# The opening of a hybrid decoder step: step sizes in two passes with high and low weights side by side, products four k tiles behind, warm-up products on a constant, banks and turns regrouped

## The chip, the cores and the metric

One Trainium2 chip, one of its cores. The time is device microseconds of one execution of the whole kernel: 2484.97 before the change, the median of three runs between 2484.46 and 2486.34.

## What is computed

One layer of a decoder that has three token mixers (a gated convolution, a Mamba-2 scan, a cross-attention into 256 memory tokens) behind one input projection, and a SwiGLU block behind them. A prompt of 1024 tokens and eight sample tokens go through the same weights. The part that this case touches is the beginning: the norm of x, its product with the columns of w_in for the step sizes dt (32 heads), for B and C and the gates z, and the norm of the memory.

```python
mem_n = rmsnorm(mem_prompt, norm_mem_w[l])
mk = (mem_n @ w_mem_k[l]).reshape(bp, MEM_LEN, ATTN_HEADS, ATTN_HEAD_DIM)
...
sc_b, sc_c, sc_x, z, xbc, dt_raw, q, gates = jnp.split(xn @ w_in, splits, axis=-1)
xbc_c, ssm_conv_new = causal_depthwise_conv(xbc, ssm_hist, ssm_conv_w)
xbc_c = jax.nn.silu(xbc_c + ssm_conv_b)
xs, bm, cm = jnp.split(xbc_c, [SSM_D_INNER, SSM_D_INNER + SSM_GROUPS * SSM_STATE], axis=-1)
dt = jax.nn.softplus(dt_raw.astype(jnp.float32) + ssm_dt_bias.astype(jnp.float32))
a = -jnp.exp(ssm_a_log.astype(jnp.float32))
acum = jnp.cumsum((dt * a).reshape(bsz, nc, q, ng, hpg), axis=2)
```

## The kernel before

All products are f32 in value: every operand is split into a high part in the format fp32r and a low part (the rest, fp32r as well), and a product is three passes over PE, high x high, high x low and low x high. A weight block is 128 columns of w_in by 1024 rows, loaded as one tile of 128 x 1024 (tag raw), cast to high by ACT (whi) and subtracted to low by DVE (wlo). The names end in r, h and l: wdtr, wdth, wdtl. The activations xn are eight k tiles (128 rows of the model dimension) of 1032 tokens, xnh and xnl, and every product over all tokens comes as three column groups of 256, 512 and 264 (FULL).

**The order** on each engine is fixed when the program is built: a scheduler walks the program in the order in which it is written, each engine then works through its own queue in order, and semaphores tie the queues together. The loads and stores of SP have eight semaphores in turn, so each waits for the one eight places earlier. Where the program calls `in_turn`, the casts, the subtractions and the loads of weights stay in the order in which they are written.

**The opening**, to which the change belongs:

1. Constants: ident, ones (128 x 128 in f32, L94), tri.
2. Three of the eight x tiles are loaded, then the small parameter rows, then the weights of dt (wdtr, L493; 128 columns are loaded although dt has 32 heads) and of B0 (wB0r), then the other x tiles.
3. `square` and `root_of`: sums of squares by ACT, the inverse root by DVE and ACT, spread over partitions by PE (ps_rb) and copied to rbc.
4. A loop over three token groups (384, 384, 264 tokens) and eight k tiles. `blocks` transposes x into ps_xt (PE, L529), and `to_xn` copies it to xt (ACT, L510; three buffers), sends xt to xT_d in DRAM (SP, L511), scales it to xw (DVE, L513), casts xnh (ACT, L514) and subtracts xnl (DVE, L515). `first_products` adds the products of dt and B0 into ps_dt and ps_B, for token group g - 1 while group g is transposed; each k tile has six products, three for dt and three for B0.
5. Behind the loop: the histories of the convolutions are transposed (ps_h) and copied (h_xc, h_sc); the first linear combination for the later Strassen products is cast (T10ah, T10al, L406); ps_dt gets its bias and becomes dtr (DVE, L606); ps_B is copied to uB (ACT, L794); then `gemm` writes ps_C (C0), and `z_step(0)` and `z_step(1)` write ps_z, each followed by a silu on ACT (z, L815).
6. `gemm` calls `tick` several times in a product of 24 x 3 matmuls; `pace[0]` (3) says how many times. Each tick takes the next piece of a list, `pend`: the softplus of dt (`dt_softplus`, transposes ps_dtT), cumulative sums ps_ac (L647), their transposes ps_acT with the exponentials eaT (L669), the rows of the sample (ps_ex, L690), the norm of the memory (`mem_rms`), its transposes (`mem_t`, ps_mt, L1241: two pieces of two halves each, each half with four transposes and then four casts and four subtractions), the keys and values (`kv_block`).
7. From Z2 on, pairs of column blocks are computed by `strassen` (L302) in seven products of half the size, with `st_prod` (L261), in three PSUM tiles with the tags m0, m1 and m2. Z2 and Z4 are the first two.

PSUM has eight banks. ps_dt, ps_B and each ps of a gemm take three banks; m0, m1 and m2 two banks each. A tile waits for whoever last used its banks.

```python
tags = ("m0", "m1", "m2") if count[0] % 2 == 0 else ("m2", "m1", "m0")
...
pa, pb = (st_ps(t, f"{nm}{t}") for t in tags[:2])
...
n = int(pace[0] + pace[1])
pace[1] += pace[0] - n
marks = [nk * i // n for i in range(n)]
```

## Time and profile before

| | |
|---|---|
| median of three runs | 2484.97 us |
| the profiled execution | 2481.99 us, its span 2480.1 us |
| busy share of PE, PEld, DVE, ACT, POOL | 98%, 93%, 64%, 43%, 5% |
| granted clock of PE, mean over the span | 0.996 |
| PE busy in 0 to 60 us | 0.81, 6.80, 8.08, 8.87, 10.00 and 9.26 of each 10 |
| PE busy in 160 to 280 us | 120.00 of 120 |

PE is matmul, PEld weight load, DVE the vector engine, ACT the scalar engine, POOL gpsimd, SP the queue of loads and stores. The profile is read stage by stage: the busy share of PE says little about the first 160 us, which are the only ones in which PE waits for other engines. In a row of the timeline stand the start and the length of a run of like instructions, the engine, the line, the operation, the output, the inputs, the shape and their number; in brackets stands the idle time ahead of it and what ended it. The table of windows gives busy time by engine, and the chain of waits names what was last at each step.

### The profile page before, as it was taken

How to read it: one execution, taken by the hardware profiler on the slowest of the kernel's cores; microseconds unless marked ns; L12 is line 12 of the kernel's file. 1: busy time of each engine (PE TensorE's matmuls, PEld its weight loads, DVE VectorE, ACT ScalarE, POOL GpSimd, SP SyncE). 2: the span in 40 equal slices, each digit the busy share in tenths (PEclk: the TensorE clock that was granted, in tenths of full speed). 3: DMA queues.
4: the chain of work that ended last, by engine and by line, in shares of the span. 5: the costliest groups of instructions: out<-in, count | busy, mean ns of one | idle time of the engine just before them, and what ended most of it. 6: DMA issues, size and time to landing. Idle time of an engine off the chain costs nothing.

```text
span 2480.1 us, 45608 instructions
## 1 busy us (share of the span) xinstructions
PE 2426.3 (98%) x18906; PEld 2308.0 (93%) x18906; DVE 1587.2 (64%) x2598; ACT 1072.3 (43%) x1716; POOL 118.3 (5%) x163
## 2 busy tenths in 40 slices
PE   7999999999999999999999989999999999999998
PEld 5899999999999999888888877899999999999998
DVE  5754587777678774656767562454787555476755
ACT  6553455454555535556545441213453333342322
...
GB/s 199 107 128 171 121 104 154 126 114 120 136 129 140 128 160 205 182 207 262 264 225 286 205 257 236 256 249 154 133 176 145 99 95 112 69 224 144 154 86 69
DMA packets 359661, 404.80 MB, mean 163 GB/s; under 512 B 16422, under 2 KB 286870, under 8 KB 359447
## 3 DMA queue, kind: packets, MB, share of 16 engines
...
## 4 chain that ended last, share of the span: by engine, by line
PE 86%; DMA 6%; DVE 4%; ACT 2%; issue 1%; SPq 0%; ACTq 0%; POOL 0%; DVEq 0%
PE po L215 12%; PE pm L1755 4%; PE ps_q L215 3%; PE pd L215 1%; PE py L998 1%; PE ps_g L215 1%; PE pss L1011 1%; PE po L990 1%; PE Z2m L261 1%; PE C3m L261 1%; PE G18m L261 1%; PE Z14m L261 1%; PE C6m L261 1%; PE G12m L261 1%; PE C4m L261 1%
## 5 line engine op out<-in xcount | busy, mean ns | idle before, releaser
L943 ACT ACTIVATE r<-r,acum 128x128 f32<-128x128 f32 x256 | 79.2, 392 | 4.1 <-DMA r<-ac_d 3.6
L714 DVE SCALAR_TENSOR_TENSOR ax<-u,prm,ax 128x1024 f32<-128x1024 f32 x44 | 56.3, 1280 | 0.1
L975 POOL TENSOR_TENSOR xdd<-xdt,decst 128x512 f32<-128x512 f32 x32 | 38.9, 1215 | 288.8 <-DVE xdt L971 288.8
L884 ACT ACTIVATE st<-st,es 128x128 f32<-128x128 f32 x128 | 41.6, 393 | 22.6 <-DMA st<-in_state_ssm_dram 18.5
L1402 DVE TENSOR_TENSOR yr<-po,yr 128x1032 f32<-128x1032 f32 x8 | 9.8, 1230 | 55.8 <-PE po L215 45.8
L994 DVE TENSOR_TENSOR y<-po,ea 128x512 f32<-128x512 f32 x28 | 19.3, 689 | 37.2 <-PE po L990 37.2
L969 DVE TENSOR_TENSOR r<-r,cbm 128x1024 f32<-128x1024 f32 x32 | 39.2, 1224 | 2.7 <-ACT bT L968 0.5
L886 DVE SCALAR_TENSOR_TENSOR st<-sr,dts,st 128x128 f32<-128x128 f32 x128 | 40.1, 344 | 0.4
L968 ACT COPY bT<-bp 128x128 f32<-128x128 f32 x32 | 8.5, 265 | 69.9 <-DVE cbm L966 69.7
L1989 ACT ACTIVATE fj<-psy 128x512 f32<-128x512 f32 (+1 forms) x18 | 10.7, 595 | 58.9 <-PE psy L1987 58.8
L890 DVE SCALAR_TENSOR_TENSOR sr<-st,sr 128x128 f32<-128x128 f32 x128 | 35.1, 284 | 1.1
L998 PE MATMUL py<-r,xdt 128*64 128x128 f32 x512 | 35.0, 279 | 0.0
L944 ACT ACTIVATE r<-r 128x1024 f32<-128x1024 f32 x32 | 33.8, 1058 | 0.6
L971 DVE TENSOR_TENSOR xdt<-xp,dtT 128x512 f32<-128x512 f32 x32 | 21.9, 685 | 18.6 <-PE xp L964 18.4
L1011 PE MATMUL pss<-xdd,bT 128*128 128x512 f32 x64 | 33.4, 603 | 0.3 <-ACT bT L968 0.3
L1762 DVE TENSOR_TENSOR x<-pm,xT 128x516 f32<-128x516 f32 x16 | 11.1, 695 | 35.1 <-PE pm L1755 35.1
L998 PEld LDWEIGHTS py<-r,xdt 128*64 128x64 f32 x512 | 27.3, 137 | 4.1 <-issue 0.5
L990 PE MATMUL po<-bc,s 128*128 128x128 f32 x224 | 29.8, 276 | 1.0 <-DVE s L1017 1.0
L1024 POOL TENSOR_TENSOR s<-s,cdec 128x512 f32<-128x512 f32 x28 | 30.2, 1078 | 7.4 <-DVE s L1017 7.0
L990 PEld LDWEIGHTS po<-bc,s 128*128 128x128 f32 x224 | 27.6, 191 | 2.8 <-issue 1.6
L1684 DVE TENSOR_TENSOR gt<-po,gt 128x1032 f32<-128x1032 f32 x8 | 9.9, 1232 | 30.0 <-PE po L215 28.2
L717 DVE SCALAR_TENSOR_TENSOR ax<-u,prm,ax 128x1032 f32<-128x1032 f32 x22 | 28.3, 1287 | 0.0
...
## 6 DMA issues: line engine op xcount, KB each, us to landing
...
```

Of the source, the lines that this page charges most:

```text
L215: PE.matmul(out[:, c : c + n], wt[:, ks], x[:, c : c + n], start=(k == 0 and i == 0), stop=(k == nk - 1 and i == 2),)
L261: PE.matmul(hv(ps)[:, c : c + n], wt[:, ks], x[:, c : c + n], start=(start and kt == 0 and i == 0), stop=(kt == 3 and i == 2), skip_group_ ...
L714: V.scalar_tensor_tensor(acc[:, :T], u[:, j : j + T], w[j], acc[:, :T], op0=ALU.mult, op1=ALU.add)
L884: S.activation(st[:, i], st[:, i], AF.Copy, scale=es[:, g * 4 + i, b : b + 1])
L886: V.scalar_tensor_tensor(st[:, i], rb, dts[:, g * 4 + i, b : b + 1], st[:, i], op0=ALU.mult, op1=ALU.add)
L943: S.activation(r[:, j, :], r[:, j, :], AF.Relu, scale=-1.0, bias=acum[:, c, h : h + 1])
L969: V.tensor_tensor(r, r, bc(cbm.unsqueeze(1), [P, HPG, P]), op=ALU.mult)
L975: G.tensor_tensor(b3(xdd, HPG), b3(xdt, HPG), bc(decst[:, c, hs].unsqueeze(2), [P, HPG, 64]), op=ALU.mult)
L990: PE.matmul(po[:, t * P : (t + 1) * P], state["s"][:, t * P : (t + 1) * P], bcg[1][:, cs], start=True, stop=True,)
L998: PE.matmul(py[hp : hp + 64, (h // 2) * P : (h // 2 + 1) * P], xdt[:, h * 64 : (h + 1) * 64], r[:, (h % 2) * 4 + h // 2, :], start=True, s ...
L1011: PE.matmul(pss, bT, xdd, start=True, stop=True)
L1755: PE.matmul(hv(ps)[:, c : c + n], wt[:, ks], x[:, half * HT + c : half * HT + c + n], start=(k == 0 and i == 0), stop=(k == KD - 1 and i = ...
```

## The change

- On PE, 32 products of `ones` with itself (128 x 128, f32) stand ahead of everything else; their result, in a PSUM tile called warm, is not used.
- The weights of dt are loaded with their 32 columns only. High and low stand side by side in one tile, 64 columns per k tile. dt is two passes then, (high and low) x xnh and (high and low) x xnl, and the 64 rows of the result are high and low parts: dtr has 64 rows, the transposes of it are 64 wide (ps_dtT and, for the sample, ps_dtS), and DVE adds the two halves. The result contains the low x low term too, which was left out before. The raw load of B0's weights is issued where it was, their casts follow in `first_weights`, called in the loop at group 0 and k tile 2.
- `first_products` becomes `dt_product` (two matmuls) and `b_product` (three). They are put into a queue, which is taken from with each k tile, from the fifth on: they follow the transposes by four k tiles instead of eight. The B products of the last group stand behind the loop.
- xt has five buffers instead of three.
- The tags of Strassen's tiles: m2, m1, m0 for Z2 (m0, m1, m2 before), m1, m2, m0 for Z4 (m2, m1, m0 before).
- The four halves of `mem_t` are four pieces of `pend` instead of two, and `pace[0]` is 5 during `z_step(1)`, 3 elsewhere.

```diff
--- before.py
+++ after.py
@@ -98,6 +98,10 @@
         base=0, channel_multiplier=-1,
     )
 
+    warm = sm_ps("warm")
+    for _ in range(32):
+        PE.matmul(warm[:, :P], ones, ones, start=True, stop=True)
+
     root = cp.tile([P, 1], F32, tag="root", name="root")
     S.activation(root, ones[:, 0:1], AF.Sqrt)
 
@@ -328,7 +332,12 @@
             raw1, raw2 = lead[0], st_raw(src2, f"{nm}r2")
         elif ready is None and early is None:
             raw1, raw2 = st_raw(src1, f"{nm}r1"), st_raw(src2, f"{nm}r2")
-        tags = ("m0", "m1", "m2") if count[0] % 2 == 0 else ("m2", "m1", "m0")
+        if count[0] == 0:
+            tags = ("m2", "m1", "m0")
+        elif count[0] == 1:
+            tags = ("m1", "m2", "m0")
+        else:
+            tags = ("m0", "m1", "m2") if count[0] % 2 == 0 else ("m2", "m1", "m0")
         count[0] += 1
         pa, pb = (st_ps(t, f"{nm}{t}") for t in tags[:2])
 
@@ -493,8 +502,18 @@
         def par(key, i):
             return prm[:, PC[key] + i : PC[key] + i + 1]
 
-        w_dt = weights(wblock(w_in, C_DT), "wdt")
-        w_b0 = weights(wblock(w_in, C_XBC + 16 * P), "wB0")
+        raw_dt = wp.tile([P, 1024], F32, tag="raw", name="wdtr")[:, : KD * HEADS].rearrange("p (k c) -> p k c", k=KD)
+        in_turn("raw", SY.dma_start(raw_dt, w_in[:, C_DT : C_DT + HEADS].rearrange("(k p) c -> p k c", p=P)))
+        w_b0 = []
+        loaded["wB0"] = load_raw(wblock(w_in, C_XBC + 16 * P), "wB0")
+        w_dt = wp.tile([P, 1024], F32R, tag="whi", name="wdt")[:, : 2 * KD * HEADS]
+        w_dt = w_dt.rearrange("p (k c) -> p k c", k=KD)
+
+        def first_weights():
+            in_turn("hi", S.copy(w_dt[:, :, :HEADS], raw_dt))
+            in_turn("lo", V.tensor_sub(w_dt[:, :, HEADS:], raw_dt, f32(w_dt)[:, :, :HEADS]))
+            w_b0.extend(weights(None, "wB0"))
+
         st = p0.tile([P, 9], F32, tag="st", name="st")
         rst = p0.tile([P, 9], F32, tag="rst", name="rst")
         V.memset(st, 1.0)
@@ -506,7 +525,7 @@
 
         def to_xn(k, c, ps, n, name):
             hi, lo = xn[k]
-            xt = p0.tile([P, 384], F32, tag="xt", bufs=3, name="xt" + name)
+            xt = p0.tile([P, 384], F32, tag="xt", bufs=5, name="xt" + name)
             S.copy(xt[:, :n], ps[:, :n])
             SY.dma_start(xT_d[k, :, c], xt[:, :n])
             xc = xw[k][:, c]
@@ -540,15 +559,27 @@
             c, n_all = span(g3)
             V.tensor_copy(rbc[:, c], ps[:, :n_all])
 
-        def first_products(g3, k):
+        def dt_product(g3, k):
+            cw = slice(FULL[g3][0], sum(FULL[g3]))
+            for i, x in enumerate(xn[k]):
+                PE.matmul(
+                    flat(ps_dt)[: 2 * HEADS, cw], w_dt[:, k, :], x[:, cw],
+                    start=(k == 0 and i == 0), stop=(k == KD - 1 and i == 1),
+                )
+
+        def b_product(g3, k):
             cw = slice(FULL[g3][0], sum(FULL[g3]))
             ah, al = xn[k]
             ks = slice(k * P, (k + 1) * P)
-            for ps, (wh, wl) in ((ps_dt, w_dt), (ps_b0, w_b0)):
-                PE.matmul(flat(ps)[:, cw], wh[:, ks], ah[:, cw], start=(k == 0), stop=False)
-                PE.matmul(flat(ps)[:, cw], wh[:, ks], al[:, cw], start=False, stop=False)
-                PE.matmul(flat(ps)[:, cw], wl[:, ks], ah[:, cw], start=False, stop=(k == KD - 1))
-
+            for i, (w, x) in enumerate(((w_b0[0], ah), (w_b0[0], al), (w_b0[1], ah))):
+                PE.matmul(
+                    flat(ps_b0)[:, cw], w[:, ks], x[:, cw], start=(k == 0 and i == 0), stop=(k == KD - 1 and i == 2)
+                )
+
+        products = deque()
+        for g3 in range(2):
+            products.extend(lambda g3=g3, k=k: [f(g3, k) for f in (dt_product, b_product)] for k in range(KD))
+        products.extend(lambda k=k: dt_product(2, k) for k in range(KD))
 
         for i in range(3):
             square(0, i)
@@ -562,12 +593,16 @@
                 if g3 < 2 and 1 <= k < 1 + len(srcs[g3 + 1]):
                     with tc.issue_after(ins):
                         square(g3 + 1, k - 1)
-                if g3:
-                    first_products(g3 - 1, k)
+                if g3 == 0 and k == 2:
+                    first_weights()
+                if g3 > 0 or k > 3:
+                    products.popleft()()
                 if g3 < 2 and k == 5:
                     root_of(g3 + 1)
+        while products:
+            products.popleft()()
         for k in range(KD):
-            first_products(2, k)
+            b_product(2, k)
 
         SY.dma_start(r_d, rbc[0:1, :])
 
@@ -600,10 +635,11 @@
 
     dt_stack = ExitStack()
     pd_ = dt_stack.enter_context(tc.tile_pool(name="pdt", bufs=1))
-    bias = pd_.tile([HEADS, 1], F32, tag="bias", name="bias")
-    SY.dma_start(bias, a["ssm_dt_bias"].rearrange("l h -> h l"))
-    dtr = ev_tile("dtr", (HEADS, TT))
-    V.tensor_scalar(dtr[:, :TT], flat(ps_dt)[:HEADS], bias, None, op0=ALU.add)
+    bias = pd_.tile([2 * HEADS, 1], F32, tag="bias", name="bias")
+    V.memset(bias, 0.0)
+    SY.dma_start(bias[:HEADS], a["ssm_dt_bias"].rearrange("l h -> h l"))
+    dtr = ev_tile("dtr", (2 * HEADS, TT))
+    V.tensor_scalar(dtr[:, :TT], flat(ps_dt)[: 2 * HEADS], bias, None, op0=ALU.add)
     W = 9 * HEADS
 
     def small(name):
@@ -617,11 +653,17 @@
     def dt_softplus():
         ps = sm_ps("ps_dtT")
         for c in range(NCK):
-            PE.transpose(ps[:, c * HEADS : (c + 1) * HEADS], dtr[:, c * P : (c + 1) * P], ident[:HEADS, :HEADS])
-        PE.transpose(ps[:NS, 256:288], dtr[:, T:TT], ident[:HEADS, :HEADS])
+            PE.transpose(
+                ps[:, c * 2 * HEADS : (c + 1) * 2 * HEADS], dtr[:, c * P : (c + 1) * P], ident[: 2 * HEADS, : 2 * HEADS]
+            )
+        pss = sm_ps("ps_dtS")
+        PE.transpose(pss[:NS, : 2 * HEADS], dtr[:, T:TT], ident[: 2 * HEADS, : 2 * HEADS])
         V.memset(x0[:, 256:], 0.0)
-        V.tensor_copy(x0[:, :256], ps[:, :256])
-        V.tensor_copy(x0[:NS, 256:], ps[:NS, 256:288])
+        for dst, src in ((x0[:, :256], ps), (x0[:NS, 256:], pss[:NS, : 2 * HEADS])):
+            dst = dst.rearrange("p (c h) -> p c h", h=HEADS)
+            src = src.rearrange("p (c t h) -> p c t h", t=2, h=HEADS)
+            V.tensor_copy(dst, src[:, :, 0])
+            V.tensor_tensor(dst, src[:, :, 1], dst, op=ALU.add)
         V.tensor_scalar(mx, x0, 0.0, None, op0=ALU.max)
         V.scalar_tensor_tensor(u, x0, -1.0, x0, op0=ALU.mult, op1=ALU.min)
         S.activation(u, u, AF.Exp)
@@ -1275,9 +1317,11 @@
 
     mem_load()
     pend.extend([None, mem_rms, None])
-    pend.extend(lambda m=m: [mem_t(m, half) for half in range(2)] for m in range(2))
+    pend.extend(lambda m=m, half=half: mem_t(m, half) for m in range(2) for half in range(2))
     pend.extend(lambda j=j, q=q: kv_block(j, q) for j in range(8) for q in range(2))
+    pace[0] = 5
     z_step(1)
+    pace[0] = 3
 
     def plain3():
         for kt in range(4):
```

Where instructions move, and where: first the PE at the beginning of the loop, with the third transposed k tile (three x tiles each into ps_xt) and the first products. Before:

```order
L529 MATMUL ps_xt_238<-ident,x_150 128x128
L529 MATMUL ps_xt_238<-ident,x_152 128x128
L529 MATMUL ps_xt_238<-ident,x_154 128x128
L548 MATMUL ps_dt<-xnh_121,wdth 128x256
L548 MATMUL ps_B_146<-xnh_121,wB0h 128x256
L549 MATMUL ps_dt<-xnl_122,wdth 128x256
L550 MATMUL ps_dt<-xnh_121,wdtl 128x256
L549 MATMUL ps_B_146<-xnl_122,wB0h 128x256
L550 MATMUL ps_B_146<-xnh_121,wB0l 128x256
```

and after (the number in a name tells tiles of one name apart; wdt holds high and low):

```order
L548 MATMUL ps_xt_264<-ident,x_183 128x128
L548 MATMUL ps_xt_264<-ident,x_185 128x128
L548 MATMUL ps_xt_264<-ident,x_187 128x128
L565 MATMUL ps_dt<-xnh_154,wdt 64x256
L565 MATMUL ps_dt<-xnl_155,wdt 64x256
L575 MATMUL ps_B_179<-xnh_154,wB0h 128x256
L575 MATMUL ps_B_179<-xnl_155,wB0h 128x256
L548 MATMUL ps_xt_281<-ident,x_183 128x128
L548 MATMUL ps_xt_281<-ident,x_185 128x128
```

The products of the first k tile stand behind the third transposed tile in both; in the changed program it has two products for dt instead of three, both ahead of B0, and its B0 products are split: low x high comes behind the next tile's transposes.

Second, ACT right behind the loop, where the last xnh are cast and the products of C0 need their weights. Before:

```order
L514 CAST xnh_135<-xw_144 128x264
L163 CAST wz0h<-wz0r 128x1024
L406 CAST T10ah<-xw_137 128x516
L406 CAST T10ah<-xw_138 128x516
L163 CAST wz1h<-wz1r 128x1024
L794 COPY uB_717<-ps_B_146 128x1032
L639 ACT_TABLE_LOAD
L639 ACTIVATE abc<-abc 128x32
```

and after:

```order
L533 CAST xnh_168<-xw_177 128x264
L415 CAST T10ah<-xw_170 128x516
L415 CAST T10ah<-xw_171 128x516
L167 CAST wC0h<-wC0r 128x1024
L167 CAST wz0h<-wz0r 128x1024
L836 COPY uB_726<-ps_B_179 128x1032
L681 ACT_TABLE_LOAD
L681 ACTIVATE abc<-abc 128x32
L753 ACTIVATE aB_730<-uB_726,prm 128x1024
L167 CAST wz1h<-wz1r 128x1024
```

wC0h, cast inside the loop before (at 39.80 us in the profile), now stands behind both casts of T10ah; wz1h has moved behind uB and aB. On SP, the loads wC0r and wz0r stand behind the last xT_d now, and stood among the xT_d of the second and third group before. On DVE, in the same place, before:

```order
L622 MEMSET x_701 128x32
L586 COPY h_xc<-ps_h_0_637 128x192
L586 COPY h_xc<-ps_h_8_649 128x192
L164 TENSOR_TENSOR wz0l<-wz0r,wz0h 128x1024
L586 COPY h_xc<-ps_h_16_661 128x192
L586 COPY h_sc<-ps_h_0_673 128x128
L606 TENSOR_SCALAR dtr<-ps_dt,bias 32x1032
L712 TENSOR_SCALAR aB_721<-h_xc,prm 128x8
L407 TENSOR_TENSOR T10al<-xw_137,T10ah 128x516
```

and after:

```order
L621 COPY h_xc<-ps_h_0_645 128x192
L621 COPY h_xc<-ps_h_8_657 128x192
L621 COPY h_xc<-ps_h_16_669 128x192
L621 COPY h_sc<-ps_h_0_681 128x128
L639 MEMSET bias 64x1
L661 MEMSET x_710 128x32
L416 TENSOR_TENSOR T10al<-xw_170,T10ah 128x516
L416 TENSOR_TENSOR T10al<-xw_171,T10ah 128x516
L168 TENSOR_TENSOR wC0l<-wC0r,wC0h 128x1024
L642 TENSOR_SCALAR dtr<-ps_dt,bias 64x1032
```

dtr now has wC0l and both T10al ahead of it, and in the changed program the first product of C0 on PE waits for dtr and for wC0h; in the program before it waits for uB.

Third, ACT around the silu of z(1), for which the first product of Z2 waits in both programs. Before:

```order
L406 CAST xnh_127<-raw_888 128x516
L669 ACTIVATE eaT<-ps_acT_925 32x512
L815 ACT_TABLE_LOAD
L815 ACTIVATE z_1178<-ps_z_1093 128x1032
L669 ACT_TABLE_LOAD
L669 ACTIVATE eaT<-ps_acT_932 32x512
L816 DMA zs_d<-z_1178 128x1032
L248 CAST Z2Sh<-Z2sa 128x1024
```

and after:

```order
L415 CAST xnh_160<-raw_900 128x516
L711 ACTIVATE eaT<-ps_acT_937 32x512
L711 ACTIVATE eaT<-ps_acT_944 32x512
L857 ACT_TABLE_LOAD
L857 ACTIVATE z_1216<-ps_z_1105 128x1032
L252 CAST Z2Sh<-Z2sa 128x1024
L858 DMA zs_d<-z_1216 128x1032
```

Both eaT stand ahead of z now; one table load is gone between them, and Z2Sh follows z directly. From the third product of Z4 on the order of PE is the same in both programs, as are ACT's and DVE's queues from there.

## The prediction

> **What bounds the kernel now.** I read the table of windows first, because the page's 98% for PE is an average. Its columns are the busy time of PE, PEld, DVE, ACT and POOL in each stretch, then the granted PE clock, the DMA share and GB/s.
>
> ```profile
> 20.00:30.00 10.00, 8.08 (x48) 6.14 (x47) 6.27 (x15) 5.65 (x15) 0.00 (x0) 1.00 0.43 154
> 40.00:50.00 10.00, 10.00 (x52) 7.31 (x51) 8.57 (x19) 5.83 (x14) 0.00 (x0) 1.00 0.70 199
> 100.00:110.00 10.00, 7.37 (x48) 6.90 (x46) 7.05 (x11) 7.24 (x11) 0.00 (x0) 0.83 0.46 133
> 130.00:140.00 10.00, 6.34 (x53) 5.90 (x52) 7.60 (x17) 9.62 (x25) 0.00 (x0) 1.00 0.27 108
> ...
> 160.00:220.00 60.00, 60.00 (x514) 60.00 (x513) 25.90 (x30) 24.14 (x34) 0.00 (x0) 1.00 0.51 161
> ```
>
> PE has holes up to 140 us, and from 160 on it is full: 60.00 of 60. The order of PE differs between the two programs only up to the beginning of Z4 (from the row Z4m<-xnh,Z4Th on it is the same). So the sum is one number, **how much earlier Z4 is reached**, which a PE that waits for nobody carries to the end. The next question is what the holes before Z4 wait for. The chain of waits (start, length, what) names it:
>
> ```profile
> 12.23 1.04 ACT wdth L163
> ...
> 54.94 4.32 DMA xT_d<-xt
> 59.35 1.14 ACT T10ah L406 x2
> 60.50 0.95 ACT wz1h L163
> 61.45 0.92 ACT uB L794
> 62.41 5.53 PE ps_C L215 x18
> 68.85 8.69 PE ps_C L215 x54
> ```
>
> Four points divide the opening: X, the end of the last xt copy on ACT (54.91 before: 54.53 + 0.38 in a row below); the first ps_C product, 62.41, which is X + 7.5; the start of Z2; the start of Z4. The last two rows also show a ps_C product at 0.31 us (5.53 / 18) and then at 0.16 (8.69 / 54): a stretch of PE at half rate, with PE at work all the time.
>
> **Warm products.**
>
> ```profile
> 1.07 0.27 DVE L465 MEMSET rows<- 128x256 f32 x1
> 8.78 0.44 PE L490 MATMUL ps_prm<-ident,rows 128*128 128x128 f32 x1 [8.78 <-DVE rs_v L110]
> 10.79 1.54 PE L529 MATMUL ps_xt<-ident,x 128*128 128x128 f32 x6
> 13.19 0.85 ACT L510 COPY xt<-ps_xt 128x384 f32<-128x384 f32 x2
> 1007.10 1.05 PE L990 MATMUL po<-bc,s 128*128 128x128 f32 x8
> 1008.08 1.09 PE L998 MATMUL py<-r,xdt 128*64 128x128 f32 x16
> ```
>
> The constant is written when the next memset starts, at 1.07, and PE is empty until 8.78. A 128x128 matmul in f32 shows as two rows: eight rows took 1008.08 - 1007.10 = 0.98, so 0.245 us a matmul at full clock. At half clock I take 0.43, since a pair of 256-wide rows goes from 0.24 to 0.43 below. All 32 at full clock end at 1.1 + 7.8 = 8.9, all at half clock at 1.1 + 13.8 = 14.9. The half-rate stretches in this trace last 3.3 to 5.5 us (rows above and below); with 5 us (12 matmuls) and 20 at 0.245 the block ends at **W = 11.0**, the value I take. From ps_prm's start to the xt transposes it is 2.0, half of 1.54 for the first three of them is 0.8, and some 0.2 of waiting for rst falls away: first xt at W + 2.6 = 13.6, **0.4 us later** than 13.19.
>
> **The loop to X.** Each k tile loses one product of ps_dt (five products instead of six).
>
> ```profile
> L510 ACT COPY xt<-ps_xt 128x384 f32<-128x384 f32 (+1 forms) x24 | 10.2, 442 | 8.7 <-PE ps_xt L529 5.6 <-DMA xT_d<-xt 1.5 <-issue 1.3
> 14.45 0.61 DVE L513 SCALAR_TENSOR_TENSOR xw<-ps_xt,prm,rbc 128x384 f32<-128x384 f32 x1
> 15.10 0.51 ACT L514 CAST xnh<-xw 128x384 fp32r<-128x384 f32 x1
> 54.53 0.38 ACT L510 COPY xt<-ps_xt 128x264 f32<-128x264 f32 x1 [0.85 <-PE ps_xt L529]
> ```
>
> At full clock 256 columns cost 0.12 us (the pairs of 0.24 below), 512 twice that, 264 about the same as 256. The 512- and 264-wide products lie where PE is full (10.00 of 10 in 40 to 50): 8 x 0.24 + 8 x 0.12 = **2.9 us**. The 256-wide ones lie where PE is busy 8.08 of 10: I count nothing for them. Five xt buffers instead of three take away xt's wait for xT_d, **1.5 us** in the group's row. The casts of 1024 columns (1.04 on ACT, one on DVE behind it) no longer stand ahead of the first xw: xw could end at 13.19 + 0.43 + 0.61 = 14.2 and xnh start at 14.4 where it started at 15.10: **0.7 us**. X moves by 2.9 + 1.5 + 0.7 - 0.4 = 4.7, to **50.2**. Bounds: 1.8, if the chain from xt over xw to xnl, and not PE, sets the pace once PE is lighter; 7.7, if W is 8.9 (1.7 better than 0.4 later: 2.1) and the 256-wide ones count too (0.9).
>
> **From X to ps_C.** Here the change costs something. Behind X ACT casts T10ah twice and then wC0h; DVE does T10al, wC0l and dtr. ps_C now gets the PSUM banks that ps_dt held, so its first product waits for dtr where it waited for uB.
>
> ```profile
> 7.49 4.72 DMA wdtr<-in_w_in_dram
> 59.40 0.34 SPq L604 DMA_DIRECT2D bias<-in_ssm_dt_bias_dram  x1
> 61.74 1.27 DVE L606 TENSOR_SCALAR dtr<-ps_dt,bias 32x1032 f32<-32x1032 f32 x1
> 65.83 1.27 DVE L714 SCALAR_TENSOR_TENSOR aB<-uB,prm,aB 128x1024 f32<-128x1024 f32 x1
> ```
>
> Step by step: 4.4 until xT_d has landed (54.91 to 59.35, kept), 1.15 for T10ah twice, 0.95 for wC0h (wz1h's length), 1.15 for wC0l (the like on DVE), 1.2 for dtr: X + 8.9, where it was X + 7.5. wC0r's load is queued on SP behind the last xT_d now; issued at about X + 0.5 and taking wdtr's 4.72, it lands at X + 5.2, under T10ah. The bias is issued when xT_d has landed and the history copies are done, about X + 5.5; before, it took under 61.74 - 59.74 = 2.0 us, so it hides behind wC0l, which ends at X + 7.7. Each us by which one of them outlasts its cover is a us more. ps_C starts at 50.2 + 8.9 = 59.1: **3.3 us earlier**. dtr on 64 rows costs what it cost on 32 (128 rows of aB also took 1.27). The two extra sums on DVE cost at most a few tenths, and PE has 187 products behind ps_C, 30 us at 0.16, as cover.
>
> **From ps_C to Z2.**
>
> ```profile
> 101.62 0.59 ACT L669 ACTIVATE eaT<-ps_acT 32x512 f32<-32x512 f32 x1 [0.80 <-DVE acT L668]
> 102.22 1.28 ACT L815 ACT_TABLE_LOAD   x1
> 103.51 1.03 ACT L815 ACTIVATE z<-ps_z 128x1032 f32<-128x1032 f32 x1
> 104.60 0.51 PE L261 MATMUL Z2m<-xnh,Z2Ah 128*128 128x256 f32 x2 [2.63 <-ACT z L815]
> ```
>
> The tags of Z2 are regrouped, but banks go by first use: its first tile lands where z(1) stands, and still waits for ACT's z. What helps is pace 5: the sums ps_ac stand 10 products earlier (187 rows behind ps_C's start, 197 before), 1.6 us at 0.16. Then both eaT stand ahead of z, which gives 0.5 back. PE idles 1.5 instead of 2.6: **1.1 us** (0 if DVE's queue, not PE, sets ps_ac; 1.6 if the second eaT hides).
>
> **From Z2 to Z4.**
>
> ```profile
> 106.14 0.64 PE L261 MATMUL Z2m<-xnh,Z2Ah 128*128 128x256 f32 x2
> 106.57 0.63 PE L261 MATMUL Z2m<-xnl,Z2Ah 128*128 128x256 f32 x2
> 109.56 0.41 PE L261 MATMUL Z2m<-xnh,Z2Al 128*128 128x256 f32 x2
> 109.80 0.40 PE L261 MATMUL Z2m<-xnh,Z2Ah 128*128 128x256 f32 x2
> 117.65 0.66 PE L690 MATMUL ps_ex<-ident,exs 8*128 8x8 f32 x8
> 123.38 0.80 PE L261 MATMUL Z2m<-xnh,Z2Th 128*128 128x256 f32 x2
> 126.69 0.39 PE L261 MATMUL Z2m<-xnh,Z2Th 128*128 128x256 f32 x2
> 135.16 1.09 PE L1241 MATMUL ps_mt<-ident,mem 128*128 128x128 f32 x8 [3.16 <-DVE meml L1246]
> ```
>
> The transposes of the memory come as four pieces, the first two ahead of the last eight products of Z2 (0.12 each, 0.95), and ACT loads one table fewer (1.28) ahead of them. That meets the 3.16 us of waiting; I take **1.0** (0 to 2.2). Then there are two stretches at half rate, 106.14 to 109.56 and 123.38 to 126.69, each 3.4 us and so 1.7 lost. The first follows an idle of 2.63; with 1.5 I let it go: **1.7** (0 if it stays, 3.4 if both go). The second follows the small transposes of ps_ex, which stand where they stood, and stays.
>
> The Trainium skill, "TensorE: Matmul & The Clock Gate", Part 1, has the clock fall to half after an idle window of about 3.4 us that runs free of the kernel, and its Part 4 says that transposes do not count as busy in the same way. The trace shows half rate after only 2.63 us of idle and after ps_ex, so it bears out Part 4 and is stricter than Part 1. By that page the warm block brings the first products nothing, as only transposes stand between it and them; worked out from its figures (an estimate) W is 1.1 + 3.4 + 24 x 0.245 = 10.4 and the first products run at half clock as before, within half a us of the sum here.
>
> **The sum.** 3.3 + 1.1 + 1.0 + 1.7 = 7.1 us. The profiled execution took 2481.99 (span 2480.1), which gives 2474.9; it lies 3.0 under the median of the three runs, 2484.97, and against that I forecast **2477.9**. What a measurement of this kernel tells from no change is about 0.2%, 5 us: faster is under 2480.0, slower over 2489.9.
>
> **The rivals.**
> - *The warm block runs at half clock to its end.* W = 14.9; for it speaks the 5.53 us of half rate in ps_C, with PE at work. X comes 3.9 later than I take it and the gain is 3.2: 2481.8. Chance 0.20.
> - *Everything comes in:* W = 8.9 and both half-rate stretches gone, 2.1 + 1.7 more: gain 10.9, 2474.1. Against it: ps_ex stays where it was. Chance 0.14.
> - *The change doesn't do what it says:* the bank change removes no wait (Z2 still waits for z), and ps_C waits for dtr behind the loads of wC0r and bias. With X only 1.8 earlier (53.1) and the loads 2 us over their cover, ps_C starts at 53.1 + 10.9 = 64.0, 1.6 later than before; with 1.1 + 1.0 from the later terms 0.5 is left: 2484.5. Chance 0.09.
> - *Slower:* the f32 block does not overlap its weight loads with its products. At half clock, a load as long as its product, 32 x 0.86 = 27.5 and W = 28.6; all behind moves 17.6 later than I take it: 2495.5. It decides from W = 23 on (12 us over 11.0, where 7 of gain become 5 of loss). The 0.98 for eight rows, loads included, speaks against it. Chance 0.06.
> - The forecast itself keeps 0.51; most of its own spread, 2 us either way from X, stays under 2480.0.
>
> **How the numbers follow.** Faster: 0.51 + 0.14 = 0.65. Within 0.2%: 0.20 + 0.09 = 0.29. Slower: 0.06. The range 2473.5 to 2483.5 holds the forecast, the half-clock block and the best case, 0.85 less their outer edges; it leaves out the slower rival and most of the third.
>
> **What the changed profile would show.** Right: the warm rows end near 11, their spacing falling from 0.21 to 0.12; xt waits for no xT_d; the last xt ends near 50.2; ps_C starts near 59.1, released by DVE dtr; Z2 starts after an idle near 1.5, released by ACT z, with no half rate in its first product; the waits of ps_mt together are near 2. Wrong: warm rows beyond 13; ps_C released by a load, or over 9.5 behind the last xt; half rate in Z2's first product; or a gain at Z4 that is gone at the end, which would mean that some later wait hangs on a load and not on PE.

## The result, and the profile after

| | before | after |
|---|---|---|
| median of 14 runs | 2482.82 us | 2478.60 us |
| lowest and highest | 2479.44, 2486.34 | 2471.28, 2481.63 |
| the profiled execution, and its span | 2481.99, 2480.1 | 2481.63, 2479.3 |
| mean granted clock of PE | 0.996 | 0.993 |

The ratio is 0.9981, with a 95% interval of 0.9973 to 0.9989: 4.7 us faster, between 2.7 and 6.7. That is the forecast's direction and within its range, at two thirds of the 7.1 us that it summed up. The two profiled executions stand only 0.8 us apart in span, though the changed kernel is over 6 us ahead when 500 us have passed. Here the choice of the execution counts: that of the changed kernel is the slowest of its 14, whose spans run from 2468.9 to 2479.3, and that of the kernel before lies 0.8 under its median. So two questions are left: did the opening gain what the sum said and for the reasons it gave, and where did the rest go?

The table of windows of the changed kernel, the same stretches as before (busy time of PE, PEld, DVE, ACT and POOL, PE clock, DMA share, GB/s):

```profile
20.00:30.00 10.00, 8.11 (x50) 5.72 (x50) 7.72 (x20) 6.50 (x16) 0.00 (x0) 1.00 0.44 152
40.00:50.00 10.00, 9.91 (x59) 7.32 (x60) 9.44 (x22) 6.16 (x17) 0.00 (x0) 1.00 0.38 126
...
100.00:110.00 10.00, 10.00 (x88) 9.84 (x87) 5.38 (x6) 3.81 (x6) 0.00 (x0) 1.00 0.39 114
110.00:120.00 10.00, 10.00 (x76) 9.53 (x77) 5.85 (x14) 5.57 (x11) 0.00 (x0) 0.83 0.37 106
120.00:130.00 10.00, 7.49 (x54) 6.54 (x54) 6.45 (x17) 7.95 (x17) 0.00 (x0) 0.93 0.27 108
130.00:140.00 10.00, 10.00 (x77) 9.85 (x76) 5.30 (x12) 7.02 (x21) 0.00 (x0) 0.90 0.17 52
160.00:220.00 60.00, 60.00 (x513) 60.00 (x512) 26.51 (x30) 25.45 (x35) 0.00 (x0) 1.00 0.51 163
```

The stretches from 100 and from 130 are full, where they were 7.37 and 6.34 of 10; but the one from 120 holds 7.49, and it was full before. So the hole ahead of Z4 is smaller and comes earlier, but it is still there. The loop (20 to 30) is as full as it was, on 50 rows instead of 48. The clock of 0.83 has moved from 100-110 to 110-120, and 130-140 shows 0.90 where it was 1.00: the half rate did not go, it stands elsewhere.

The chain of waits has the warm products as one piece, and the timeline of PE shows the landmarks (start, length, engine, line, what, and in brackets the idle time ahead and its releaser):

```profile
1.12 9.60 PE warm L103 x64
```

```profile
10.55 0.27 PE L499 MATMUL ps_prm<-ident,rows 128*128 128x128 f32 x1
...
58.22 1.20 PE L219 MATMUL ps_C<-xnh,wC0h 128*128 128x256 f32 x3 [4.25 <-ACT uB L836]
99.26 0.51 PE L265 MATMUL Z2m<-xnh,Z2Ah 128*128 128x256 f32 x2 [1.73 <-ACT z L857]
127.47 0.66 PE L1283 MATMUL ps_mt<-ident,mem 128*128 128x128 f32 x4 [2.12 <-DVE meml L1288]
128.27 0.54 PE L265 MATMUL Z4m<-xnh,Z4Ah 128*128 128x256 f32 x2
129.48 0.58 PE L265 MATMUL Z4m<-T10ah,Z4Sh 128*128 128x256 f32 x1 [0.23 <-ACT Z4Sh L252]
```

ACT's timeline gives the first and the last copies of xt, and the first row of half rate in the loop stands on PE:

```profile
12.55 0.86 ACT L529 COPY xt<-ps_xt 128x384 f32<-128x384 f32 x2 [2.13 <-PE ps_xt L548]
48.32 0.88 ACT L529 COPY xt<-ps_xt 128x264 f32<-128x264 f32 x2
```

```profile
15.45 0.28 PE L575 MATMUL ps_B<-xnl,wB0h 128*128 128x256 f32 x1
...
16.91 0.41 PE L575 MATMUL ps_B<-xnh,wB0h 128*128 128x256 f32 x1
```

The block ends at 10.72 and the last xt (X) at 49.20. One matmul of 256 columns takes 0.28 at 15.45 and 0.41 at 16.91: the clock falls to half again 5 us behind the end of the block.

In all runs below I read six points: X; the first ps_C; the first product of Z2; the first product X4m<-T40ah,X4Dh (X4 for short), which stands for "the opening is over"; the end of the span; and the time from X4 to the end. PE's rows stand in one order in both kernels from Z4m<-xnh,Z4Tl on (158.18 before, 151.32 after), and X4 lies some 342 us behind it. In e9 and e12 the common order begins at 282 and 283, and in every run well ahead of X4.

| run | X | ps_C | Z2 | X4 | end | X4 to end | ratio (95%) |
|---|---|---|---|---|---|---|---|
| before | 54.91 | 62.41 | 104.60 | 500.35 | 2480.1 | 1979.7 | 1 |
| after | 49.20 | 58.22 | 99.26 | 494.03 | 2479.3 | 1985.3 | 0.9981 (0.9973 to 0.9989) |
| e1 no warm block | 51.23 | 60.91 | 100.83 | 493.51 | 2477.2 | 1983.7 | 0.9985 (0.9975 to 0.9994) |
| e2 warm block alone | 56.05 | 63.16 | 105.38 | 501.59 | 2481.8 | 1980.2 | 0.9999 (0.9990 to 1.0008) |
| e3 three xt buffers | 55.50 | 63.78 | 103.87 | 491.98 | 2473.3 | 1981.4 | 0.9971 (0.9960 to 0.9983) |
| e4 loads and bias early | 48.99 | 52.97 | 103.99 | 493.65 | 2473.6 | 1980.0 | 0.9978 (0.9965 to 0.9991) |
| e5 memory norm early | 50.03 | 59.05 | 101.50 | 493.33 | 2473.9 | 1980.5 | 0.9974 (0.9964 to 0.9984) |
| e6 old turns | 49.44 | 58.58 | 99.68 | 494.01 | 2478.9 | 1984.9 | 0.9979 (0.9970 to 0.9988) |
| e7 four buffers, norm early | 50.59 | 58.34 | 102.76 | 497.44 | 2481.8 | 1984.4 | 0.9991 (0.9981 to 1.0001) |
| e8 a third pass for dt | 51.19 | 58.71 | 109.97 | 502.25 | 2484.6 | 1982.4 | 0.9997 (0.9988 to 1.0007) |
| e9 norm behind z | 49.82 | 58.84 | 98.68 | 492.06 | 2471.3 | 1979.3 | 0.9968 (0.9955 to 0.9980) |
| e10 after again | 48.60 | 57.62 | 98.35 | 492.51 | 2477.4 | 1984.9 | 0.9981 (0.9972 to 0.9990) |
| e11 old tags | 49.76 | 58.77 | 99.20 | 493.77 | 2473.4 | 1979.6 | 0.9974 (0.9963 to 0.9986) |
| e12 e9 again | 49.60 | 58.62 | 99.85 | 492.61 | 2472.8 | 1980.2 | 0.9974 (0.9965 to 0.9983) |

Ratios are of many runs against the kernel before; the points are of one profiled execution each. Two executions of one program differ by 1.5 us at X4 (after and e10), 0.7 of it from the warm block, which ends between 10.06 and 11.45 in all runs. Counted from its end, X4 comes after 482.5 to 483.5 us in the changed kernel, e6, e10 and e11, and after 480.7 to 481.5 in e3, e9 and e12; less than 1 us is not read.

### The profile page after: what moved, and what is told of

The parts are those of the page before. It is cut to its first block, busy times and chain, and to the rows that moved or that the text cites. A ratio compares the mean times of both kernels' runs of the same rounds, so it can differ in the third digit from the quotient of the medians.

```text
span 2479.3 us, 45686 instructions
## 1 busy us (share of the span) xinstructions
PE 2433.7 (98%) x18946; PEld 2312.4 (93%) x18946; DVE 1586.1 (64%) x2601; ACT 1067.9 (43%) x1714; POOL 114.3 (5%) x163
## 4 chain that ended last, share of the span: by engine, by line
PE 84%; DMA 6%; DVE 6%; ACT 2%; issue 1%; SPq 0%; ACTq 0%; DVEq 0%; POOL 0%
PE po L219 12%; PE ps_q L219 4%; PE pm L1799 4%; PE ps_g L219 2%; PE pd L219 1%; PE py L1040 1%; PE pss L1053 1%; PE po L1032 1%; PE Z2m L265 1%; PE d02m L265 1%; PE ps_z L219 1%; PE Z4m L265 1%; PE X8m L265 1%; PE C1m L265 1%; PE G18m L265 1%
## 5 line engine op out<-in xcount | busy, mean ns | idle before, releaser
L926 ACT ACTIVATE st<-st,es 128x128 f32<-128x128 f32 x128 | 41.5, 392 | 28.6 <-DMA st<-in_state_ssm_dram 23.0
L2033 ACT ACTIVATE fj<-psy 128x512 f32<-128x512 f32 (+1 forms) x18 | 10.7, 595 | 59.1 <-PE psy L2031 59.0
```

The lines of the kernel that those rows point to most:

```text
L926: S.activation(st[:, i], st[:, i], AF.Copy, scale=es[:, g * 4 + i, b : b + 1])
```

## Where the gain went behind the opening

At X4 the changed kernel is 6.3 us ahead (500.35 - 494.03), at the end 0.8. The rows of PE between are the same in both. The largest wait in the first 100 us behind X4 that the kernel before does not have is in C2. ACT of the changed kernel:

```profile
572.27 1.28 ACT L926 ACTIVATE st<-st,es 128x128 f32<-128x128 f32 x4 [4.81 <-DMA st<-in_state_ssm_dram]
573.46 1.03 ACT L252 CAST C3Ah<-C3r 128x1024 fp32r<-128x1024 f32 x1
```

Its DVE, and then its PE:

```profile
574.52 1.23 DVE L253 TENSOR_TENSOR C3Al<-C3r,C3Ah 128x1024 fp32r<-128x1024 f32 x1 [4.38 <-ACT C3Ah L252]
575.67 0.69 DVE L394 TENSOR_TENSOR su<-su,C2m 128x516 f32<-128x516 f32 x1
```

```profile
576.41 0.51 PE L265 MATMUL C2m<-T40ah,C2Dh 128*128 128x256 f32 x2 [1.27 <-DVE su L394]
```

The same ACT instructions in the kernel before, and in e9:

```profile
575.17 1.28 ACT L884 ACTIVATE st<-st,es 128x128 f32<-128x128 f32 x4 [2.36 <-DMA st<-in_state_ssm_dram]
```

```profile
568.23 1.28 ACT L926 ACTIVATE st<-st,es 128x128 f32<-128x128 f32 x4 [2.74 <-DVE c L379]
```

Read from the end backwards: PE waits 1.27 for DVE's su; DVE could not do su sooner because it stood idle for 4.38 in front of C3Al, which waited for ACT's cast C3Ah; ACT stood 4.81 in front of a scan state st that had not been loaded. In the kernel before ACT waits for the same load, but 2.36, and PE does not wait at all; in e9 the load has landed and PE does not wait there either. The load is issued on SP at 569.21, only 3.0 earlier than the 572.18 of the kernel before, while PE comes 6.3 earlier. But neither the order of the program nor an early PE settles whether this wait is there: in e12, the program of e9 run again, ACT stands 4.27 for the same load and PE 0.73, and e6 has no wait in C2 and loses as much behind X4. What the row shows is that a PE that has been full for hundreds of microseconds still does not carry its whole gain. A further wait in this stretch is 0.7 (G4m for DVE), which e9 has too.

The rest of the 5.6 us (1985.3 - 1979.7) stands in other places and not always in the same. All waits of PE behind X4 sum to 23.7 us in the changed kernel and to 20.9 in the kernel before; to that come half-rate stretches of 3.4 us at 1586 and 2241, which the kernel before does not have (1.7 lost in each). e10, the same kernel run again, has neither of these two stretches, waits 25.4 in all, and ends with the same loss.

## The experiments

**e1: the warm block left out; e2: the warm block alone, on the kernel before.**

```diff
-    warm = sm_ps("warm")
-    for _ in range(32):
-        PE.matmul(warm[:, :P], ones, ones, start=True, stop=True)
```

> The changed kernel without the 32 warm products. My theory: the block is worth little, because only transposes stand between it and the first products and PE was at half rate again from 16.0 to 19.4 us in the changed profile. Without it the first xt copy starts about 0.3 earlier than 12.55, the first products run at half rate until about 20, the last xt ends within 0.7 us of 49.2 and Z4's second T1 product within 1 us of 133.7. Rival: the block keeps the clock up and is worth 2 us or more, then the last xt ends at 51 or later.

> The kernel before with the 32 warm products and nothing else. My theory: the first xt copy waits on ACT for the cast of wdth until 13.2 in any case, so the block delays nothing and saves at most half of the half-rate stretch of the first group; Z4's second T1 product stays within 1 us of 139.8. Rival: the block is what moved the end of the loop (5.7 us earlier in the changed kernel), then most of that shows here and the last xt ends before 52.

Without the block X is 2.0 and ps_C 2.7 later than in the changed kernel, Z2 1.6, but X4 comes 0.5 earlier and the ratio is 0.9985 against 0.9981. So the rival of e1 was right at X, and nothing of that is left at X4. Alone, the block gives 0.9999 with X 1.1 later. The waits of PE in e1 (what, for how long in all, how often, the longest) show the same ones ahead of Z4 as in the changed kernel:

```profile
PE ps_C L215 <- ACT uB L832: 5.2, 1, 5.2
PE ps_mt L1279 <- DVE meml L1284: 2.1, 1, 2.1
PE Z2m L261 <- ACT z L853: 1.7, 1, 1.7
```

What differs between the two behind Z2 is one stretch of half rate, at 115.0 in the changed kernel, which e1 lacks. The block neither pays nor costs anything that these intervals tell.

**e3: three buffers for xt.**

```diff
-            xt = p0.tile([P, 384], F32, tag="xt", bufs=5, name="xt" + name)
+            xt = p0.tile([P, 384], F32, tag="xt", bufs=3, name="xt" + name)
```

> The changed kernel with three xt buffers as before. The loads of wC0, wz0 and wz1 go back among the xT_d stores on SP, and wC0's casts into the loop. By the prediction's terms xt waits for xT_d again and the last xt ends 1.5 later, at 50.7, and ps_C starts at about 59.7. The rival, which I hold for likelier now: the five buffers pushed the load of wC0 behind all stores, and ps_C waits less here behind the loop (xT_d landing 2.6, T10ah 1.15, T10al 0.65, dtr 1.2 make 5.6 to 7.4 behind the last xt instead of 9.0), so that ps_C starts at 57 or earlier although the last xt ends later.

The groups of instructions of e3, then of the changed kernel (busy time and mean | idle time ahead and what ended most of it):

```profile
L529 ACT COPY xt<-ps_xt 128x384 f32<-128x384 f32 (+1 forms) x24 | 10.2, 443 | 11.7 <-PE ps_xt L548 7.5 <-DMA xT_d<-xt 4.1
```

```profile
L529 ACT COPY xt<-ps_xt 128x384 f32<-128x384 f32 (+1 forms) x24 | 10.4, 442 | 8.7 <-PE ps_xt L548 7.0 <-ACT xnh L533 0.7 <-ACT xt L529 0.6
```

With three buffers X is 6.3 later, at 55.50, no better than before: the wait for xT_d is 4.1, more than the 1.5 of the kernel before, beside a loop with less other work. Neither expectation came true: X and ps_C are both later than either said. All of the gain at X needs the buffers; three of them also put the load and the cast of wC0 back into the loop, but e4 (below) has these there too, with five buffers, and X at 48.99. And yet e3 is ahead of the changed kernel at X4 by 2.1 (by 0.5 of its repetition e10) and has the better ratio, 0.9971, though the intervals overlap. Its waits of PE between ps_C and Z4 are two:

```profile
PE ps_C L219 <- DVE dtr L642: 4.0, 1, 4.0
PE Z2m L265 <- ACT z L857: 1.4, 1, 1.4
```

There is no wait of ps_mt, and from 67.5 to 1467 no half rate. So Z2 comes 4.6 later and X4 2.1 earlier: what lies between Z2 and X4 takes 388.1 where it takes 394.8 in the changed kernel and 395.8 before.

**e4: the loads of wC0, wz0 and wz1 put into the loop, that of the bias into the opening.**

```diff
+            loaded["wC0"] = load_raw(wblock(w_in, C_XBC + 20 * P), "wC0")
...
+                if g3 == 1 and k in (2, 5):
+                    i = (k - 2) // 3
+                    loaded[f"wz{i}"] = load_raw(wblock(w_in, C_Z + i * P), f"wz{i}")
```

and the bias gets a tile of its own, loaded ahead of the loop.

> The changed kernel with the loads of wC0, wz0 and wz1 written into the loop and the bias loaded at the start into a tile of its own, so that dtr no longer waits for the stores of xT_d. If the wait for dtr and wC0 behind the loop is what holds ps_C (9.0 us behind the last xt), ps_C starts about 3 us behind the last xt, at 52 to 53, and Z4's second T1 product comes at 131 or earlier (2.5 us or more are won). Rival: DVE is full from 60 to 90 us anyway and its work sets the sums ps_ac; then ps_C starts early but PE waits later, and Z4 stays within 1 us of 133.7.

ps_C starts 5.3 earlier than in the changed kernel, at 52.97, 4.0 behind X. Then PE stands, and Z2 is 4.7 later. A row of PE's timeline and two windows:

```profile
87.11 1.19 PE L693 MATMUL ps_ac<-da,tri 128*128 128x256 f32 x2 [5.88 <-issue]
```

```profile
60.00:90.00 30.00, 23.57 (x138) 20.21 (x138) 29.79 (x56) 17.44 (x23) 13.76 (x3) 0.89 0.27 91
83.00:93.00 10.00, 5.50 (x16) 4.25 (x17) 9.16 (x18) 3.87 (x7) 5.28 (x1) 0.51 0.50 160
```

DVE is busy 29.79 of 30 from 60 to 90, and the sums ps_ac need its da. PE, which came earlier, reaches them before DVE has it and idles 5.88: the bracket names no releaser, but da starts on DVE at 86.57, takes 0.45, and ps_ac starts at 87.11. The clock falls within that idle and stays at half from 83.3 to 93.5 (0.51 over 10 us). X4 comes within 0.4 of the changed kernel. So 5 us won at ps_C are worth nothing at X4: in this stretch **DVE's queue, not PE, is the bound** of e4. In the changed kernel da ends at 89.27 and PE reaches ps_ac at 90.57, so DVE had only 1.3 us to spare.

**e5: the norm of the memory early, in memory of its own; e7: the same with four buffers.**

```diff
-    mst = pm.tile([P, 2], F32, tag="mst", name="mst")
-    mrs = pm.tile([P, 2], F32, tag="mrs", name="mrs")
+    mst = cn.tile([P, 2], F32, tag="mst", name="mst")
+    mrs = cn.tile([P, 2], F32, tag="mrs", name="mrs")
...
-            junk = memT[m][0].rearrange("p k c -> p (k c)")
+            junk = ev_tile(f"mjunk{m}", (P, D))
```

The reason for them is in the changed kernel's ACT and DVE:

```profile
114.95 1.06 ACT L1273 ACTIVATE memh<-mem 128x1024 fp32r<-128x1024 f32 x1 [2.79 <-PE ps_ex L735]
```

```profile
121.44 0.69 DVE L397 TENSOR_TENSOR Z<-Z,Z2m 128x516 f32<-128x516 f32 x1 [1.22 <-PE Z2m L265]
122.05 0.15 DVE L118 SCALAR_TENSOR_TENSOR rs_t<-rs_v,rs_t 128x2 f32<-128x2 f32 x1
122.23 0.16 DVE L119 SCALAR_TENSOR_TENSOR mrs<-rs_t,mrs 128x2 f32<-128x2 f32 x1
```

The squares of the memory write into memory that the work on dt holds until ps_ex is done, so they start at 114.95; and the end of the inverse root (0.15 and 0.16 long) stands on DVE behind a sum of Z that waits for PE. Both make ps_mt late.

> The changed kernel with the statistics of the memory's norm in tiles that do not wait for dt's tiles to be freed (the squares go to a scratch tile). The order up to Z2 is the same; the transposes of the memory come 40 to 100 products before Z4 instead of 8. My theory: the wait of ps_mt (2.1 us) and the half-rate stretch behind it (128.6 to 132, 1.7 us) are what keeps the head start from Z2 from arriving at Z4; last xt, ps_C and Z2 stay within 0.7 us of 49.2, 58.2 and 99.3, and the first X4m<-T40ah product comes 2 to 4 us before 494.0. Rival: that product stays within 0.7 us of 494.0, because another wait or another half-rate stretch takes the place.

> Four xt buffers instead of five, which puts the load of wC0 back among the stores and its casts into the loop, together with the memory's norm as in e5. If the loop is set by the buffers, the last xt ends between 49.2 (five) and 55.5 (three); if the order behind the loop is worth what three buffers showed, ps_C comes less than 9 behind it. With the memory's wait gone the first X4m<-T40ah product should come at 488 to 491, the best of all; the total at 0.997 or below of before. Rival: what is won behind the loop is lost in it, and the product stays at 490 to 492, as in e3 or e5.

The wait of ps_mt is gone in both, and a larger one takes its place. ACT and PE of e5:

```profile
97.60 1.28 ACT L115 ACT_TABLE_LOAD   x1
98.89 0.20 ACT L115 ACTIVATE rs_t<-rs_v 128x2 f32<-128x2 f32 x1
99.12 1.28 ACT L857 ACT_TABLE_LOAD   x1
100.41 1.03 ACT L857 ACTIVATE z<-ps_z 128x1032 f32<-128x1032 f32 x1
```

```profile
101.50 0.80 PE L265 MATMUL Z2m<-xnh,Z2Ah 128*128 128x256 f32 x2 [3.83 <-ACT z L857]
```

The root of the norm stands ahead of z with a table load of its own, Z2 waits 3.83 instead of 1.73, and its first products run at half rate (from 100.4). Neither comes to the X4 that was expected: e5 is level there (0.7 ahead, which isn't read), and e7 has z later still (Z2 at 102.76), two half-rate stretches of 6.8, and loses 3.4 at X4.

**e6: the pieces of mem_t and the pace as before.**

```diff
-    pend.extend(lambda m=m, half=half: mem_t(m, half) for m in range(2) for half in range(2))
+    pend.extend(lambda m=m: [mem_t(m, half) for half in range(2)] for m in range(2))
...
-    pace[0] = 5
     z_step(1)
-    pace[0] = 3
```

> The changed kernel with the memory's transposes in two pieces of two and the pace at 3 throughout, as before the change. The prediction gave these edits 1.1 (sums ten products earlier) and 1.0 (memory's wait). The order of PE shows the sums and the first three of the memory's transposes at the same places without these edits, so I expect no loss: Z2 within 0.5 us of 99.3 and the first X4m<-T40ah product within 1 us of 494.0. Rival: it comes 2 us later or more.

X4 is 494.01 against 494.03, the ratio 0.9979 against 0.9981, and the wait of ps_mt is the same:

```profile
PE ps_mt L1283 <- DVE meml L1288: 2.1, 1, 2.1
```

PE's rows stand in the same order as in the changed kernel, from the first to the last, so these two edits move nothing on PE.

**e8: a third pass for dt, with weights of zero.**

```diff
+            PE.matmul(flat(ps_dt)[: 2 * HEADS, cw], w_no, xn[k][0][:, cw], start=False, stop=(k == KD - 1))
```

It adds 24 products of zeros and leaves the sums as they are.

> The changed kernel with a third product per k tile and group for dt, on weights of zero, so that PE has as many products in the loop as before the change (24 more, 3.8 us of PE at full clock). The prediction gave 2.9 us to their removal. By it the last xt ends at 52, 2.9 later than 49.2. Rival: PE has room in the loop once five buffers let the chain of xt, xw, xnh and xnl run (ACT and DVE set the pace), and the last xt ends within 1 us of 49.2. The order behind Z2 also moves here (the memory's transposes come earlier), so only the loop is to be compared.

X moves 2.0 later, 0.7 of it because the first xt comes at 13.28 instead of 12.55: the pass is worth 1.3 to 2.0 at X, between the two expectations. Its Z2 is 10.7 later, because ps_ac is placed where PE stands 6.8 for it, as in e4 (da ends on DVE at 93.72):

```profile
93.83 1.19 PE L693 MATMUL ps_ac<-da,tri 128*128 128x256 f32 x2 [6.76 <-issue]
```

The ratio says little about the pass, then: the placing of the sums outweighs it.

**e9: the norm's squares in memory of their own, but behind z; e12: the same once more.** The edit of e5, and

```diff
-    pend.extend([None, mem_rms, None])
+    pend.extend([None] * 5 + [mem_rms, None])
```

> As e5, but the squares of the memory are put behind z(1) on ACT (three empty turns more in front of them), since in e5 they stood ahead of z and Z2 waited 3.8 us for it. My theory: Z2 starts within 0.7 us of 99.3 with a wait of 1.7 as in the changed kernel, the memory's wait ahead of Z4 is gone, and the first X4m<-T40ah product comes at 489.5 to 492, 2 to 4.5 us before 494.0; ratio 0.9972 or below. Rival: half-rate stretches elsewhere between Z2 and Z4 take it back, and the product stays at 493 or later.

> The kernel of e9 (squares of the memory behind z), unchanged. Theory: its ratio of 0.9968 and its two readings belong to its order of work, so Z2 starts with an idle under 2.2 us, ps_mt waits for nobody, X4m<-T40ah,X4Dh stands at 493 or earlier, the later part to the end is again 1979.3 within 1, and the ratio lies under the 0.9981 of the changed kernel. Rival: the later part differs from run to run of one order, and what this order has over the changed kernel is worth less than 1 us: then the later part comes out at 1982 or more here, or the ratio at 0.9980 or above.

PE of e9:

```profile
98.68 0.51 PE L265 MATMUL Z2m<-xnh,Z2Ah 128*128 128x256 f32 x2 [1.73 <-ACT z L857]
...
125.46 0.41 PE L265 MATMUL Z4m<-xnh,Z4Ah 128*128 128x256 f32 x2
```

Z2 waits 1.73 as in the changed kernel, ps_mt waits for nobody, and Z4 begins 2.8 earlier, 0.6 of which Z2 had already. X4 comes 2.0 earlier than in the changed kernel and only 0.5 earlier than in e10; counted from the end of the warm block, e9 and e12 are 1.8 us ahead of after and e10 on average. This is the best kernel of the study by its median: 0.9968 (2473.73 us), and 0.9974 the second time (2476.13), which is 3.2 and 1.7 us better than the changed kernel's 0.9981, though the intervals overlap. X4 is at 492.06 and 492.61, the later part 1979.3 and 1980.2. The changed kernel and its repetition have 1985.3 and 1984.9 there. Each order gave nearly the same twice, but two profiles each do not show that the order is the cause, as the next runs tell.

**e10: the changed kernel again; e11: the tags as before.**

```diff
-        if count[0] == 0:
-            tags = ("m2", "m1", "m0")
-        elif count[0] == 1:
-            tags = ("m1", "m2", "m0")
-        else:
-            tags = ("m0", "m1", "m2") if count[0] % 2 == 0 else ("m2", "m1", "m0")
+        tags = ("m0", "m1", "m2") if count[0] % 2 == 0 else ("m2", "m1", "m0")
```

> The changed kernel once more, with another profile. My theory: up to the first X4m<-T40ah product it comes at 494 within 1.5 us, and from there to the end it takes anything between 1980 and 1985 us, since half-rate stretches and short waits fall at other places in each execution (the first profile has 1985.3, the kernel before 1979.7 and 1980.2 with the same order). Rival: the changed program is slower there in itself, and it takes 1984 or more again, as in three profiles so far.

> The changed kernel with Strassen's tags as before the change. By the prediction the regrouping removes no wait: Z2 waits for ACT's z with 1.7 us idle as before, starts within 0.5 us of 99.3, and the first X4m<-T40ah product comes within 1 us of 494.0. Rival: Z2 or Z4 wait longer by 1 us or more without the new tags.

e10's later part is 1984.9, so in the profiles it repeats. e11 has the old tags and the same way to X4 (493.77, Z2 waits 1.7), so the tags do nothing in the opening; its later part is 1979.6 and its ratio 0.9974 (0.9963 to 0.9986), which the interval of the changed kernel overlaps. That the new tags cost the 5 us of the later part is not shown by it: e3, e4, e5 and e9 have the new tags too and are between 1979.3 and 1981.4. Nor is it PE's order: its rows stand in the same order in the changed kernel, e6, e10 and e11, which have 1985.3, 1984.9, 1984.9 and 1979.6.

The executions without a profile speak against a fixed cost as well. The 14 of the changed kernel have spans from 2468.9 to 2479.3, and the 11 of e10 from 2473.3 to 2479.1, while X4 differs by 1.5 between their two profiles. So the later part of one program moves by several microseconds from one execution to the next, as e10's theory had it; this is worked out from the spans, since only one execution of each run has a profile. It also matters which one has it: the profiled executions of the changed kernel and of e6 are the slowest of their runs, those of e7 and e10 lie in the slower half, and those of e3, e4, e5, e9, e11 and e12, with later parts of 1979.3 to 1981.4, in the faster half (e1, with 1983.7, is the fifth of 11). Between the profiles the difference stands mostly in PE's waits behind X4, which sum to 22.5 to 25.4 us in the four profiles with a later part of 1984 and more, and to 19.0 to 20.9 in the seven under 1981. What decides which of the two an execution gets stays open.

## Why the prediction was right in sign and short of its sum

**Warm block and first xt: right, 1.0 too late.** The block ends at 10.72 (predicted 11.0), with its rows 0.21 apart up to 5.7 and 0.11 apart from there, so 4.6 us of it ran at half rate where I took 5. The first xt comes at 12.55, 0.6 earlier than before and not 0.4 later: 1.83 behind the block instead of 2.6, since ps_rb and the transposes follow at once. That the first products lose the clock again came as forecast.

**The loop: right in sum, wrong in its parts.** X is 5.7 earlier (predicted 4.7; the 1.0 is that of xt). But the sum of 2.9 for the passes, 1.5 for the wait for xT_d and 0.7 for the casts is no sum: with three buffers (e3) the others together bring nothing at X, with five the passes are worth 1.3 to 2.0 (e8). The 1.5 was the wait as it stood in the old loop; in the faster loop it grew to 4.1 where the buffers were missing. A wait's size in a row says what it costs now, not what it will cost when the work beside it shrinks.

**X to ps_C: right, by two misses that meet.** Predicted X + 8.9, measured X + 9.0. ACT of the changed kernel:

```profile
51.83 1.15 ACT L415 CAST T10ah<-xw 128x516 fp32r<-128x516 f32 x2 [1.65 <-DMA xT_d<-xt]
54.50 1.04 ACT L167 CAST wC0h<-wC0r 128x1024 fp32r<-128x1024 f32 x1 [1.52 <-DMA wC0r<-in_w_in_dram]
```

and DVE, whose dtr ends the wait of ps_C (the bracket above names uB, which ended at 58.19, 0.12 behind dtr; the program waits for dtr and wC0h, the profiles of e3, e5, e6 and e9 name dtr, and in ten profiles ps_C starts 0.15 behind dtr's end):

```profile
56.79 1.28 DVE L642 TENSOR_SCALAR dtr<-ps_dt,bias 64x1032 f32<-64x1032 f32 x1
```

xT_d landed 2.6 behind X instead of the 4.4 that I kept, so T10ah was done early; wC0r landed at X + 5.3, the X + 5.2 of the prediction, but with no cover left, and ACT waited 1.52 for it. So the cast wC0h was held by the load of wC0r and not by T10ah as I had it, and since the prediction had T10ah end at X + 5.55, the sum came out the same. The load outlasts its cover, as the prediction's third rival had it, but only because xT_d had landed sooner. The load of the bias stayed hidden: dtr follows wC0l on DVE without a gap.

**ps_C to Z2: right size, wrong cause.** The idle ahead of Z2 is 1.73 (predicted 1.5), and the stretch is 1.15 shorter (predicted 1.1). But e6, without the pace of 5, has it as short (58.58 to 99.68), with ps_ac 32.4 behind ps_C as in the changed kernel (before: 34.2). The sums do stand ten rows of PE earlier (193 behind ps_C's start instead of 203), but in e6 just as much, so not because of the pace; which of the other edits moves them was not separated.

**Z2 to Z4: this is the term that failed.** Predicted 2.7 (1.0 less waiting, 1.7 for a stretch of half rate that goes); from Z2 to the first row of the common order it is 53.6 before and 52.1 after, 1.5. The waiting came in, and more than forecast: 3.2, 0.5 and 0.6 (ps_kv) before, 2.1 and 0.2 after, though not through the four pieces (e6). The 1.7 did not. In this profile the stretch in Z2's first products went, as forecast, but another came behind the wait of ps_mt. And the shorter idle does not keep it away: e10, the same program with the same idle of 1.73, has half rate there from 99.9 to 103.3. The windows of the changed kernel, four stretches of 3.4 us:

```profile
111.60:115.00 3.40, 3.40 (x36) 2.99 (x35) 1.33 (x3) 0.61 (x2) 0.00 (x0) 0.99 0.52 145
115.00:118.40 3.40, 3.40 (x17) 3.40 (x18) 1.72 (x5) 3.38 (x8) 0.00 (x0) 0.50 0.31 84
125.20:128.60 3.40, 1.13 (x8) 0.75 (x7) 2.17 (x7) 3.24 (x10) 0.00 (x0) 1.00 0.67 277
128.60:132.00 3.40, 3.17 (x15) 2.87 (x14) 2.97 (x6) 3.38 (x11) 0.00 (x0) 0.50 0.00 0
```

Two stretches before, two after, and two in e6, e10 and e11 as well, in places that differ. I had looked for the ones that were there and asked which would go, not which remaining wait could make a new one. In the sum: 3.3 became 4.2, 1.1 became 1.15 and 2.7 became 1.5, so that the common order is reached 6.9 earlier instead of 7.1: a good number, from terms of which one was too small and one too large. Of the 6.9, 0.5 is lost just ahead of X4.

**"A PE that waits for nobody carries it to the end": wrong.** The first 160 us are not the only ones in which PE waits for other engines: in the kernel before it waits 20.9 us behind X4 too, 4.3 of it once at 1475 for ACT. In the profiled pair 5.5 of 6.3 us are lost behind X4; over all runs 4.7 are left by the ratio, about three quarters of what X4 shows. The prediction named the case among its signs of being wrong, a later wait that hangs on a load, and gave it no price. The windows 160 to 220 were full, but a full PE in one stretch says nothing of the reserve that ACT and DVE have in a later one. That the forecast of 2477.9 lies only 0.7 from the measured 2478.6 is partly luck: the gain is 2.4 less than the sum, but the kernel before also came out 2.2 faster over 14 runs than in its first three.

**Which edit the gain hangs on** is shown only in part. The kernels without the block, with three buffers, with the old tags, and with the old pace and pieces have ratios of 0.9985, 0.9971, 0.9974 and 0.9979, so none of these edits alone is needed for the 0.9981, the five buffers, which give all of X, included. The two passes of dt and the closer order of the loop were not taken out alone: e8 gives back a pass and falls to 0.9997, but its sums are placed otherwise too.

**The rivals.** The block at half clock to its end did not happen (10.72, not 14.9), nor did weight loads in a row with products (28.6). Everything coming in fell with the half rate. The rival that the bank change removes no wait of Z2 was right in that part: Z2 still waits for z, and e11 shows the tags to be worth nothing there.
